# Products of 512 columns in two stages, norms' boundary chain reordered, broadcast and last values placed later

## The chip, the cores and the metric

The kernel runs on one core of one Trainium2 chip. Its time is the device time of one launch in microseconds. TensorE multiplies matrices, with stationary weights loaded ahead of each moving operand; ScalarE and VectorE prepare operands and empty PSUM, the banks into which TensorE writes; SyncE and GpSimd issue transfers.

## The reference

Two layers, each a mixer and a feed-forward block with norms before and after, on 16 meta tokens and 256 tokens of 2048 features:

```python
for layer in range(DEPTH):
    g = norm_g[layer]
    a = rms_norm(h, g[0])
    if layer % 2 == 0:
        ...   # u = a @ ab_w_in; mix = concat(pool_mixer, s5_mixer) @ ab_w_out
    else:
        ...   # mix = dsa_mixer(a, c_w_in, c_w_out)
    h = h + rms_norm(mix, g[1])
    a = rms_norm(h, g[2])
    f = jnp.square(jax.nn.relu(a @ mlp_w1[layer])) @ mlp_w2[layer]
    h = h + rms_norm(f, g[3])
return h[:, N_META:]
```

rms_norm multiplies by 1/sqrt(mean of squares over the 2048 features + 1e-6) and by a gain. The feed-forward width is 8192. dsa_mixer projects to 16 query heads of 128, 4 heads each of keys and values, 16 index queries of 64, one index key and 16 index weights; it rotates part of queries and keys, scores each query against all keys by the index parts, keeps the 64 best allowed keys, attends over them and projects back. All in float32.

## The kernel before

Activations lie with the features on 128 partitions, 16 chunks of 272 tokens (256 in the last feed-forward block and c_out, which leave the meta tokens out). Weights come as 684 tiles of 128x1024 float32, 512 KB each. For each, Stream.next issues a transfer on SyncE's queue into one of four wraw buffers, ScalarE copies it to float32r (whi, line 82), and VectorE subtracts that to get the rest (wlo, line 83). Activations are split into a high and a low half in the same way (a, ao, f). A product is three matmuls, high by high, high by low and low by high (three, lines 181 to 183). linear walks over quarters q of the 2048 inputs and in each over groups g of 256 output features; a tile holds four chunks and both halves m of a group, so 24 matmuls. A group that takes one bank pair is an mm tile, the third and later ones of a set two sd tiles.

Each engine takes its instructions in the order in which the scheduler put them, by the order of the code and by the priorities (high_priority, issue_after).

Three residuals (residual, line 284) stand between the stages. In this text A is the one after the first mixer, B the one after the first feed-forward block, C the one after c_out. TensorE does four filler matmuls (busy, line 136; they appear twice as many in the trace, since a float32 matmul is two passes), the totals (line 232) that sum the squares over the partitions, seven fillers, then the broadcast (line 258), which spreads the root over all partitions by a diagonal matrix dg, and eight fillers. Between totals and broadcast stands the root's chain (rstd_from, line 236): a square root on ScalarE and five small operations on VectorE. Then quarter(q) adds the normalised output to h (rt, then h) and splits the next stage's activations chunk by chunk.

The norm before a stage needs the new h's squares. That stage's first set of three groups runs on activations without the root; the squares are summed on VectorE as the quarters come (sqacc), and after the set totals, root and broadcast follow in the middle of the stage, before any of its output is scaled (mlp, lines 341 to 348, and mixer1, the second mixer):

```python
with tc.high_priority(250):
    squares(4)
with tc.high_priority(60):
    ps = sums.totals(n // 4)
with tc.high_priority(250):
    r = keep_bcast(rstd_from(ps, n // 4), n // 4)
```

In the second mixer the first set are keys and half of the values (kv_out), then come the index keys, the index queries (products of 512 columns by tokens, lines 1046 to 1048), scores, the selection of 64 keys by steps of max and match_replace on VectorE (lines 1103 and 1104), the other values (line 998 transposes them), and four groups of queries with the heads' attention between them. The second stage of the last feed-forward block (tail) works by tokens with 512 columns.

## Time and profile before

| | us |
|---|---|
| median of 3 runs | 2201.54 (2201.02 to 2202.66) |
| profiled execution | 2202.15 |
| its span | 2200.4 |
| TensorE busy | 2161.2 (98%) |
| VectorE busy | 1283.2 (58%) |
| ScalarE busy | 1025.7 (47%) |
| DMA engines' mean share (q1) | 51.6% |

The mean granted clock of TensorE is 0.992 of full speed. The stages: first mixer to 320.7 us, boundary A, first feed-forward block to 1100.9, boundary B, second mixer with c_out to 1457.5, boundary C, last feed-forward block to 2191. A duration of a matmul in the trace includes its way through the array, and neighbours overlap; what one costs in a stream is the distance between starts. In the idle columns the time in brackets is what the engine stood before the row, with what released it.

### The profile page before, as it was taken

To read this page: it belongs to the slowest core of one execution; us is meant where nothing else is said; L and a number is where in the kernel's file an instruction comes from. 1 tells how busy PE (TensorE), PEld (TensorE's weight loads), DVE (VectorE), ACT (ScalarE), POOL (GpSimd) and SP (SyncE) were. 2 spreads that over 40 slices of the span, in tenths; PEclk is the share of its full clock that TensorE was granted. 3 is DMA by queue.
4 is the path that set the end of the run, shared out by engine and by line. 5 is a ranking of instruction groups with operands and counts; after the bars stand their busy time and mean duration, and the time that the engine had idled before them with its cause. 6 is when DMAs were issued, how large, how long until landed. Compare 5 with 4: busy or idle time off the path is not lost.

```text
span 2200.4 us, 38716 instructions
## 1 busy us (share of the span) xinstructions
PE 2161.2 (98%) x15974; PEld 2034.2 (92%) x15974; DVE 1283.2 (58%) x1938; ACT 1025.7 (47%) x1437; POOL 30.2 (1%) x62
## 2 busy tenths in 40 slices
PE   9998999999999999999999999999999999999998
PEld 9988899999999999999998788999889989989986
DVE  8988569544544554455495855467445545545544
ACT  6553556444443443344364455456444434434442
POOL 0111000000000000000000000000000000000000
PEclk9999999999999999999999999999999999999999
DMA  7766646555555555555355432547555555555553
GB/s 238 210 180 176 193 153 197 177 174 179 175 173 178 177 173 179 176 173 176 132 167 172 149 125 87 185 129 225 189 192 184 189 187 187 186 188 191 184 197 99
DMA packets 108736, 385.14 MB, mean 175 GB/s; under 512 B 12736, under 2 KB 14656, under 8 KB 108432
## 3 DMA queue, kind: packets, MB, share of 16 engines
q1 hardware_dynamic: 103008, 368.55, 51.6%
q0 software_dynamic: 3968, 12.75, 2.3%
q8 instruction: 125, 2.05, 0.4%
q10 hardware_dynamic: 1584, 1.38, 0.2%
q14 instruction: 51, 0.42, 0.1%
HBM read 375.35 MB, written 7.27 MB: 174 GB/s over the span
## 4 chain that ended last, share of the span: by engine, by line
PE 88%; DVE 6%; issue 3%; DMA 2%; ACT 1%; POOL 0%; SPq 0%; DVEq 0%; POOLq 0%; ACTq 0%
PE mm L183 24%; PE mm L182 24%; PE mm L181 24%; PE mm L1046 2%; PE mm L1047 2%; PE mm L1048 2%; DVE wlo L83 1%; PE sd L182 1%; PE sd L181 1%; PE sd L183 1%; DMA wraw<-wall 1%; DVE a L165 1%; DMA tz<-kd 1%; DVE h L158 1%; DVE rt L158 1%
## 5 line engine op out<-in xcount | busy, mean ns | idle before, releaser
L83 DVE TENSOR_TENSOR wlo<-wraw,whi 128x1024 fp32r<-128x1024 f32 (+1 forms) x685 | 833.4, 1218 | 732.0 <-ACT whi L82 731.2
L82 ACT ACTIVATE whi<-wraw 128x1024 fp32r<-128x1024 f32 (+1 forms) x685 | 722.2, 1055 | 981.0 <-PE mm L182 681.5
L181 PE MATMUL mm<-a,whi 128*128 128x272 f32 (+1 forms) x2608 | 746.1, 287 | 2.0 <-ACT whi L82 1.9
L183 PE MATMUL mm<-a,wlo 128*128 128x272 f32 (+1 forms) x2608 | 746.5, 286 | 0.9 <-DVE wlo L83 0.9
L182 PE MATMUL mm<-a,whi 128*128 128x272 f32 (+1 forms) x2608 | 744.3, 286 | 0.2
L181 PEld LDWEIGHTS mm<-a,whi 128*128 128x128 f32 x2608 | 490.5, 188 | 4.0 <-ACT whi L82 2.4
L183 PEld LDWEIGHTS mm<-a,wlo 128*128 128x128 f32 x2608 | 490.6, 188 | 2.0 <-DVE wlo L83 1.5
L182 PEld LDWEIGHTS mm<-a,whi 128*128 128x128 f32 x2608 | 490.7, 188 | 1.3 <-DVE a L165 0.9
L182 PE MATMUL mm<-f,whi 128*128 128x272 f32 x992 | 287.0, 289 | 0.0
L183 PE MATMUL mm<-f,wlo 128*128 128x272 f32 x992 | 285.7, 288 | 0.0
L181 PE MATMUL mm<-f,whi 128*128 128x272 f32 x992 | 283.1, 285 | 0.0
L183 PE MATMUL mm<-whi,f 128*128 128x512 f32 x480 | 189.4, 395 | 0.0
L181 PE MATMUL mm<-whi,f 128*128 128x512 f32 x480 | 189.3, 394 | 0.0
L182 PE MATMUL mm<-wlo,f 128*128 128x512 f32 x480 | 188.6, 393 | 0.0
L181 PEld LDWEIGHTS mm<-f,whi 128*128 128x128 f32 x992 | 187.3, 189 | 0.0
L183 PEld LDWEIGHTS mm<-f,wlo 128*128 128x128 f32 x992 | 186.4, 188 | 0.0
L182 PEld LDWEIGHTS mm<-f,whi 128*128 128x128 f32 x992 | 186.2, 188 | 0.0
L183 PEld LDWEIGHTS mm<-whi,f 128*128 128x128 f32 x480 | 90.2, 188 | 21.1
L182 PEld LDWEIGHTS mm<-wlo,f 128*128 128x128 f32 x480 | 90.3, 188 | 20.8
L181 PEld LDWEIGHTS mm<-whi,f 128*128 128x128 f32 x480 | 90.4, 188 | 20.4
L1046 PE MATMUL mm<-whi,a 128*128 128x512 f32 x192 | 77.7, 405 | 0.0
L1047 PE MATMUL mm<-wlo,a 128*128 128x512 f32 x192 | 76.2, 397 | 0.0
(272 smaller groups left out, 2118.9 us busy)
## 6 DMA issues: line engine op xcount, KB each, us to landing
wraw<-wall SPq DMA_DIRECT2D x683, 512.0 KB, 3.6
qd<-q POOLq DMA_DIRECT2D x8, 512.0 KB, 4.3
tz<-kd POOLq DMA_DIRECT2D x32, 128.0 KB, 6.2
h<-hT SPq DMA_DIRECT2D x7, 544.0 KB, 6.0
bc<-bc SPq DMA_DIRECT2D x8, 256.0 KB, 3.2
qr<-qd POOLq DMA_DIRECT2D x4, 512.0 KB, 6.1
qq<-qd POOLq DMA_DIRECT2D x4, 512.0 KB, 5.7
out<-acc SPq DMA_DIRECT2D x8, 256.0 KB, 2.7
```

The source lines that it names most:

```text
L82: nc.scalar.activation(out=hi[:, x], in_=src[:, x], func=AF.Copy)
L83: nc.vector.tensor_tensor(out=lo[:, x], in0=src[:, x], in1=hi[:, x].bitcast(F32), op=SUB)
L158: return vec.tensor_tensor(out=out, in0=in0, in1=in1, op=op)
L165: return vec.scalar_tensor_tensor(out=out, in0=in0, scalar=scalar, in1=in1, op0=op0, op1=op1)
L181: pe.matmul(out=o, lhsT=wh, rhs=ah, start=first, stop=False)
L182: pe.matmul(out=o, lhsT=wh, rhs=al, start=False, stop=False)
L183: st.last = pe.matmul(out=o, lhsT=wl, rhs=ah, start=False, stop=last)
L1046: pe.matmul(out=o, lhsT=ah[:, s], rhs=hi[:, w], start=q == 0 and i == 0, stop=False)
L1047: pe.matmul(out=o, lhsT=ah[:, s], rhs=lo[:, w], start=False, stop=False)
L1048: st.last = pe.matmul(out=o, lhsT=al[:, s], rhs=hi[:, w], start=False, stop=q == 7 and i == 1)
```

## The change

In the first stage of the last feed-forward block and in c_out (but for its last group) a product becomes two matmuls: high weights by both activation halves, which lie side by side, into 512 columns, and low weights by the high half into the first 256. ScalarE then copies the second 256 columns out and VectorE adds the first. At the residuals the four fillers before the totals go, the root's chain is written with the reciprocal of the mean instead of that of the root, and each h follows its rt. In the middle of the stages the last squares are put ahead of the last quarter's weights, and totals, root and broadcast are apart: the broadcast comes in the third quarter of group 3 (feed-forward), or after half of the index keys (second mixer), whose other half comes after kv_out. The last values' kv_out comes behind three quarters of the first queries.

```diff
+    def two(o, wh, wl, both, ah, first, last):
+        pe.matmul(out=o, lhsT=wh, rhs=both, start=first, stop=False, skip_group_check=True)
+        st.last = pe.matmul(out=o[:, :256], lhsT=wl, rhs=ah, start=False, stop=last, skip_group_check=True)
+    def linear(name, groups, kcs, actf, n, row0=0, col0=0, before=None, mid=None, m_outer=False,
+               wide=None):
...
+            c, ends = kcs[4 * q + i], (q == 0 and i == 0, q == nq - 1 and i == 3)
+            if wide:
+                two(pt.m(m), w[0][:, s], w[1][:, s], wide(c), actf(c)[0], *ends)
+            else:
+                three(pt.m(m)[:, :n], w[0][:, s], w[1][:, s], *actf(c), *ends)
...
-        vec.reciprocal(out=r, in_=s)
-        stt(t, r, -0.5, r, MULT, MULT)
-        tt(t, t, v, MULT)
+        vec.reciprocal(out=v, in_=v)
+        tt(r, s, v, MULT)
+        stt(t, s, -0.5, r, MULT, MULT)
         stt(r, t, 1.5, r, ADD, MULT)
...
+    def side_by_side():
+        x = [apool.tile([128, 8, T], F32R, name="a").rearrange("p (c s) t -> p c s t", s=2) for _ in range(4)]
+        return [[y[:, :, s, :] for y in x] for s in range(2)] + [x]
+    def chunk(hl, s, c, t0=0, n=None):
+        k = 16 // len(hl[s])
+        return hl[s][c // k][:, c % k, t0:t0 + (n or T - t0)]
...
-        busy(bt, 4, st.last.ins)
         ps = sums.totals(n // 4)
         busy(bt, 7, sums.end.ins)
...
-                tt(t, mix(c, k), (b if c < 2 else kept)[:, None, :].to_broadcast([128, k, n]), MULT)
-                d = tt(x, x, t, ADD)
+                with tc.issue_after(d[-1].ins) if d else nullcontext():
+                    tt(t, mix(c, k), (b if c < 2 else kept)[:, None, :].to_broadcast([128, k, n]), MULT)
+                d.append(tt(x, x, t, ADD))
                 for j in range(k):
...
+        def last_squares(q):
+            if q == 3:
+                for c in range(12, 16):
+                    sums.add(c, hx(c, t0))
+        def taken(g, pt, force=False):
+            o = {}
+            for (m, k, x), (_, _, y) in zip(pt.spans(n), pt.spans(n, 256 if wide else 0)):
+                if force or wide:
+                    o[g, m] = tmp.tile([128, 2, T], F32, name="rl", tag="t2", bufs=4)[:, :k, :n]
+                    copy(o[g, m], y if wide else x)
+                    if wide:
+                        tt(o[g, m], o[g, m], x, ADD)
+            return o
...
+        def out1(g, pt, raws, fh, fl):
+            raws = raws or taken(g, pt)
+            for m, k, x in pt.spans(n):
+                c = 2 * g + m
+                rb = r[0][:, None, :n].to_broadcast([128, k, n])
+                rl = raws[g, m] if raws else tmp.tile([128, 2, T], F32, name="rl", tag="t2", bufs=4)[:, :k, :n]
+                stt(rl, rl if raws else x, 0.0, rb, MAX, MULT)
...
-            sets = [[0, 1, 2]] + [[g] for g in range(3, 8)] if b == 0 else [[g] for g in range(8)]
-            for gs in sets:
-                pts = linear(w1, gs, range(16), aget, n, col0=b * 2048, before=squares if r is None else None)
+            if b == 0:
+                gs = [0, 1, 2]
+                pts = linear(w1, gs, range(16), aget, n, before=squares, mid=last_squares, wide=wide)
+                ps = ps1()
+                with tc.high_priority(250):
+                    root = rstd_from(sums.totals(n // 4, ps=ps), n // 4)
                 raws = {}
-                if r is None:
-                    for g, pt in zip(gs, pts):
-                        for m, k, x in pt.spans(n):
-                            raws[g, m] = tmp.tile([128, 2, T], F32, name="rl", tag="t2", bufs=4)[:, :k, :n]
-                            act.activation(out=raws[g, m], in_=x, func=AF.Relu)
-                    with tc.high_priority(250):
-                        squares(4)
-                    with tc.high_priority(60):
-                        ps = sums.totals(n // 4)
-                    with tc.high_priority(250):
-                        r = keep_bcast(rstd_from(ps, n // 4), n // 4)
                 for g, pt in zip(gs, pts):
-                    for m, k, x in pt.spans(n):
-                        c = 2 * g + m
-                        rb = r[:, None, :n].to_broadcast([128, k, n])
-                        if raws:
-                            rl = raws[g, m]
-                            tt(rl, rl, rb, MULT)
-                        else:
-                            rl = tmp.tile([128, 2, T], F32, name="rl", tag="t2", bufs=4)[:, :k, :n]
-                            stt(rl, x, 0.0, rb, MAX, MULT)
-                        act.activation(out=rl, in_=rl, func=AF.Square)
-                        split(fh[c // 8][:, c % 8:c % 8 + k, :n], fl[c // 8][:, c % 8:c % 8 + k, :n], rl)
+                    raws.update(taken(g, pt, True))
+                def spread(q):
+                    if q == 2:
+                        with tc.high_priority(250), tc.issue_after(st.last.ins):
+                            r.append(keep_bcast(root, n // 4, ps))
+                        for g, pt in zip(gs, pts):
+                            out1(g, pt, raws, fh, fl)
+                pt, = linear(w1, [3], range(16), aget, n, col0=0, before=spread, wide=wide)
+                out1(3, pt, None, fh, fl)
+            for g in range(4 if b == 0 else 0, 8):
+                pt, = linear(w1, [g], range(16), aget, n, col0=b * 2048, wide=wide)
+                out1(g, pt, None, fh, fl)
...
+        pts = linear("c_in", gs, range(16), aget, T, col0=2048, before=squares, mid=last_squares)
+        rbank, xbank = ps1(), ps1()
         with tc.high_priority(250):
-            squares(4)
-        with tc.high_priority(60):
-            ps = sums.totals(T // 4)
-        with tc.high_priority(250):
-            rb = keep_bcast(rstd_from(ps, T // 4), T // 4)
-        rq = small.tile([128, 2], F32, name="rq", bufs=1)
-        vec.tensor_copy(rq, rstd_from(sums.totals(128, META, 2), 128, 2))
+            root = rstd_from(sums.totals(T // 4, ps=rbank), T // 4)
+        xk = xbank[:, :T]
+        def index_keys(x):
+            hi, lo = st.next(("c_in", 1024 * x, 8, 4096, 80), 640)
+            for i in range(8):
+                ah, al = aget(8 * x + i)
+                three(xk[:80, :], hi[:, 80 * i:80 * i + 80], lo[:, 80 * i:80 * i + 80], ah, al,
+                      x == 0 and i == 0, x == 1 and i == 7)
+        index_keys(0)
+        with tc.high_priority(250), tc.issue_after(st.last.ins):
+            rb = keep_bcast(root, T // 4, rbank)
...
+        index_keys(1)
+        rq = small.tile([128, 2], F32, name="rq", bufs=1)
+        vec.tensor_copy(rq, rstd_from(sums.totals(128, META, 2), 128, 2))
+        tt(KI[0:64], xk[0:64, :], rb[0:64], MULT)
+        tt(KI[64:80], xk[64:80, :], rb[64:80], MULT)
...
-        kv_out(3, pt)
-        for _ in project(0):
+        first_queries = project(0)
+        for _ in range(3):
+            next(first_queries)
+        with tc.issue_after(st.last.ins):
+            kv_out(3, pt)
+        for _ in first_queries:
...
-            pt, = linear("c_out", [g], range(16), lambda c: ao[c], 256, m_outer=g == 7)
+            wide = None if g == 7 else lambda c: ao[c]
+            pt, = linear("c_out", [g], range(16), lambda c: (ao[c][:, 0], ao[c][:, 1]), 256, m_outer=g == 7, wide=wide)
             c = 2 * g
+            o = mix[c // 8][:, c % 8:c % 8 + 2, :256]
             for m in range(2):
-                sums.add(c + m, pt.m(m)[:, :256])
-                copy(mix[c // 8][:, c % 8 + m, :256], pt.m(m)[:, :256], scale=g_t[:, 1, 1, c + m:c + m + 1])
+                x = pt.m(m)[:, :256]
+                if wide:
+                    copy(o[:, m], pt.m(m)[:, 256:])
+                    tt(o[:, m], o[:, m], x, ADD)
+                    x = o[:, m]
+                sums.add(c + m, x)
+                copy(o[:, m], x, scale=g_t[:, 1, 1, c + m:c + m + 1])
...
-    a = act_tiles()
+    a = side_by_side()
     quarter = residual(1, 1, mix, sums, META, to_next(1, 2, a, META))
```

On TensorE in the middle of the last block's first stage; sd tiles are the set's third group, and the four matmuls with ones and sqacc are the totals, the one with dg the broadcast. Before:

```order
L181 MATMUL mm<-a,whi 128x256
L182 MATMUL mm<-a,whi 128x256
L183 MATMUL mm<-a,wlo 128x256
L232 MATMUL sd<-ones,sqacc 64x1 x4
L181 MATMUL sd<-a,whi 128x256
L182 MATMUL sd<-a,whi 128x256
...
L183 MATMUL sd<-a,wlo 128x256
L258 MATMUL sd<-dg,ones 128x256
L181 MATMUL sd<-a,whi 128x256
```

and after:

```order
L188 MATMUL sd<-a,wlo 128x256
L187 MATMUL sd<-a,whi 128x512
L242 MATMUL sd<-ones,sqacc 64x1 x4
L188 MATMUL sd<-a,wlo 128x256
L187 MATMUL sd<-a,whi 128x512
...
L188 MATMUL mm<-a,wlo 128x256
L269 MATMUL sd<-dg,ones 128x256
L187 MATMUL mm<-a,whi 128x512
L188 MATMUL mm<-a,wlo 128x256
```

Eighteen matmuls stand between totals and broadcast in the first piece and 43 in the second, 11 of the set and 32 of group 3.

On TensorE around the transposes of the last values (vt) in the query products. Before:

```order
L1046 MATMUL mm<-whi,a 128x512
L1047 MATMUL mm<-wlo,a 128x512
L998 MATMUL sd<-ident,vt 128x128 x2
L998 MATMUL sd<-ident,vt 16x128
L998 MATMUL sd<-ident,vt 128x128 x2
L998 MATMUL sd<-ident,vt 16x128
L1048 MATMUL mm<-whi,a 128x512
L1046 MATMUL mm<-whi,a 128x512
```

and after:

```order
L1096 MATMUL mm<-whi,a 128x512
L1097 MATMUL mm<-wlo,a 128x512
L1098 MATMUL mm<-whi,a 128x512
L1053 MATMUL sd<-ident,vt 128x128 x2
L1053 MATMUL sd<-ident,vt 16x128
L1053 MATMUL sd<-ident,vt 128x128 x2
L1053 MATMUL sd<-ident,vt 16x128
L1096 MATMUL mm<-whi,a 128x512
L1097 MATMUL mm<-wlo,a 128x512
```

Of the 96 query matmuls that follow the group's last product, 14 stand ahead of these transposes before, and 72 after.

On VectorE at boundary C, the root's chain from nv on, the diagonal and the first chunks (numbers are of tiles; acc is c_out's output). Before:

```order
L171 TENSOR_SCALAR nv_15906<-sd_15886 64x4
L241 RECIPROCAL nr_15908<-ns_15907 64x4
L165 SCALAR_TENSOR_TENSOR nt_15909<-nr_15908 64x4
L158 TENSOR_TENSOR nt_15909<-nt_15909,nv_15906 64x4
L165 SCALAR_TENSOR_TENSOR nr_15908<-nt_15909,nr_15908 64x4
L158 TENSOR_TENSOR dg_15916<-ident_96,nr_15908 64x256
L158 TENSOR_TENSOR rt_15943<-acc_14844,sd_15881 128x256
L158 TENSOR_TENSOR rt_15948<-acc_14844,sd_15881 128x256
L158 TENSOR_TENSOR h_3477<-h_3477,rt_15943 128x256
L158 TENSOR_TENSOR h_3477<-h_3477,rt_15948 128x256
L158 TENSOR_TENSOR rt_15954<-acc_14844,rb_15927 128x2x256
L165 SCALAR_TENSOR_TENSOR a_15879<-h_3477,g_t_89,a_15877 128x256 x2
```

and after:

```order
L171 TENSOR_SCALAR nv_15680<-sd_15660 64x4
L252 RECIPROCAL nv_15680<-nv_15680 64x4
L158 TENSOR_TENSOR nr_15682<-ns_15681,nv_15680 64x4
L165 SCALAR_TENSOR_TENSOR nt_15683<-ns_15681,nr_15682 64x4
L165 SCALAR_TENSOR_TENSOR nr_15682<-nt_15683,nr_15682 64x4
L158 TENSOR_TENSOR dg_15690<-ident_96,nr_15682 64x256
L158 TENSOR_TENSOR rt_15717<-acc_14818,sd_15659 128x256
L158 TENSOR_TENSOR h_3477<-h_3477,rt_15717 128x256
L158 TENSOR_TENSOR rt_15722<-acc_14818,sd_15659 128x256
L158 TENSOR_TENSOR h_3477<-h_3477,rt_15722 128x256
L165 SCALAR_TENSOR_TENSOR a_15655<-h_3477,g_t_89,a_15655 128x256
L158 TENSOR_TENSOR rt_15728<-acc_14818,rb_15701 128x2x256
```

The reciprocal takes nv now and not ns, each h stands behind its rt, and the low half a of the first chunk stands ahead of the third rt.

## Rows read from the trace of the kernel before

**Rows 1.** page, part 1: busy us (share of span) xinstructions of each engine

```profile
PE 2161.2 (98%) x15974; PEld 2034.2 (92%) x15974; DVE 1283.2 (58%) x1938; ACT 1025.7 (47%) x1437; POOL 30.2 (1%) x62
```

**Rows 2.** timeline of TensorE, narrow products: start us, duration us, engine, line, operation

```profile
2039.76 0.28 PE L181 MATMUL mm<-a,whi 128*128 128x256 f32 x1
...
2047.91 0.28 PE L181 MATMUL mm<-a,whi 128*128 128x256 f32 x1
```

**Rows 3.** timeline of TensorE, last feed-forward block's second stage

```profile
1579.61 0.40 PE L183 MATMUL mm<-whi,f 128*128 128x512 f32 x1
...
1595.59 0.40 PE L183 MATMUL mm<-whi,f 128*128 128x512 f32 x1
```

**Rows 4.** groups by form: busy us, mean ns | idle before, by releaser

```profile
L82 ACT ACTIVATE whi<-wraw 128x1024 fp32r<-128x1024 f32 x679 | 719.2, 1060 | 978.3 <-PE mm L182 681.5 <-PE mm L183 188.8 <-PE mm L1048 60.5
```

**Rows 5.** timeline of TensorE, first queries and the values' transposes

```profile
1225.62 0.40 PE L1046 MATMUL mm<-whi,a 128*128 128x512 f32 x1
...
1226.56 0.40 PE L1047 MATMUL mm<-wlo,a 128*128 128x512 f32 x1
1229.45 0.74 PE L998 MATMUL sd<-ident,vt 128*128 128x128 f32 x5 [2.50 <-DVE vt L158]
```

**Rows 6.** timeline of ScalarE, middle of the last block's first stage

```profile
1495.23 1.06 ACT L82 ACTIVATE whi<-wraw 128x1024 fp32r<-128x1024 f32 x1 [4.46 <-DMA wraw<-wall]
1496.20 0.58 ACT L343 ACTIVATE rl<-mm 128x512 f32<-128x512 f32 x1
```

**Rows 7.** timeline of VectorE in the query stage

```profile
1228.58 0.72 DVE L158 TENSOR_TENSOR vt<-mm,rb 128x544 f32<-128x544 f32 x1
```

**Rows 8.** timeline of VectorE, middle of the first block's first stage

```profile
361.29 1.22 DVE L83 TENSOR_TENSOR wlo<-wraw,whi 128x1024 fp32r<-128x1024 f32 x1 [1.16 <-ACT whi L82]
```

**Rows 9.** timeline of TensorE at boundary A

```profile
322.06 1.12 PE L232 MATMUL sd<-ones,sq 128*68 128x1 f32 x16
323.04 1.81 PE L141 MATMUL sd<-ones 128*128 128x128 f32 x14
```

**Rows 10.** timeline of ScalarE at boundary A

```profile
321.38 0.43 ACT L220 ACTIVATE sq<-acc 128x272 f32<-128x272 f32 x1 [0.51 <-DVE acc L158]
```

**Rows 11.** timeline of VectorE at boundary B

```profile
1102.05 2.49 DVE L83 TENSOR_TENSOR wlo<-wraw,whi 128x1024 fp32r<-128x1024 f32 x2 [0.48 <-ACT whi L82]
```

**Rows 12.** timeline of TensorE at boundary C

```profile
1457.46 1.05 PE L141 MATMUL sd<-ones 128*128 128x128 f32 x8
1458.45 0.63 PE L232 MATMUL sd<-ones,sqacc 128*64 128x1 f32 x8
...
1464.90 0.39 PE L182 MATMUL mm<-a,whi 128*128 128x256 f32 x1
```

**Rows 13.** timeline of ScalarE at boundary C

```profile
1457.66 0.38 ACT L220 ACTIVATE sq<-sd 128x256 f32<-128x256 f32 x1 [0.68 <-PE sd L183]
```

**Rows 14.** timeline of VectorE at boundary C

```profile
1460.34 0.15 DVE L171 TENSOR_SCALAR nv<-sd 64x4 f32<-64x4 f32 x1 [9.02 <-ACT ns L239]
1460.41 0.16 DVE L241 RECIPROCAL nr<-ns 64x4 f32<-64x4 f32 x1
1460.61 0.15 DVE L165 SCALAR_TENSOR_TENSOR nt<-nr 64x4 f32<-64x4 f32 x1
...
1462.43 0.75 DVE L158 TENSOR_TENSOR rt<-acc,sd 128x256 f32<-128x256 f32 x2 [0.84 <-PE sd L258]
```

**Rows 15.** timelines of TensorE at the totals in the middle of three stages

```profile
363.01 0.62 PE L232 MATMUL sd<-ones,sqacc 128*68 128x1 f32 x8 [1.41 <-DVE sqacc L158]
...
1141.08 0.62 PE L232 MATMUL sd<-ones,sqacc 128*68 128x1 f32 x8 [0.42 <-DVE sqacc L158]
...
1146.07 0.70 PE L258 MATMUL sd<-dg,ones 68*128 68x272 f32 x2 [0.76 <-DVE dg L158]
...
1498.03 0.60 PE L232 MATMUL sd<-ones,sqacc 128*64 128x1 f32 x8 [2.19 <-DVE sqacc L158]
```

**Rows 16.** stretches of the span: length, busy of PE PEld DVE ACT POOL, PEclk, DMA

```profile
364.00:368.00 4.00, 4.00 (x22) 4.00 (x22) 3.40 (x9) 2.53 (x4) 0.00 (x0) 0.57 0.88 280
```

More of the change, by code (lines that the diff above doesn't have):

```diff
@@ L183, in three @@
         st.last = pe.matmul(out=o, lhsT=wl, rhs=ah, start=False, stop=last)
-    def linear(name, groups, kcs, actf, n, row0=0, col0=0, before=None, mid=None, m_outer=False):
+    def two(o, wh, wl, both, ah, first, last):
[3 more added lines that the diff above has]
+               wide=None):
         pts = [Pair(i < 2 and not m_outer) for i in range(len(groups))]
@@ L224, in add, with totals @@
                 self.squares.append(sq)
-        def totals(self, w, t0=0, runs=4):
-            ps = ps1()
+        def totals(self, w, t0=0, runs=4, ps=None):
+            ps = ps or ps1()
             parts = [self.acc] + self.squares
@@ L259, in bcast, with keep_bcast @@
         return ps[:, :4 * w]
-    def keep_bcast(r, w):
+    def keep_bcast(r, w, ps=None):
         o = small.tile([128, T], F32, name="rb", bufs=2)
-        copy(o[:, :4 * w], bcast(r, w))
+        copy(o[:, :4 * w], bcast(r, w, ps))
         return o
@@ L295, in residual @@
         kept = small.tile([128, T], F32, name="rb", bufs=2)[:, :n]
+        d = []
         def quarter(q):
@@ L308, in quarter @@
                 if c == 0:
-                    st.hold = (first, a and a.ins, d.ins)
+                    st.hold = (first, a and a.ins, d[0].ins)
         return quarter
@@ L315, in mlp @@
         aget = acts(a, t0, n)
-        r = None
+        wide = (lambda c: a[2][c // 4][:, c % 4, :, t0:]) if len(a) == 3 else None
+        r = []
         sums = Sums(n, 0)
@@ L326, in squares @@
         def squares(q):
-            if q < 4:
-                quarter(q)
+            quarter(q)
             for c in range(max(0, 4 * q - 4), 4 * q):
                 sums.add(c, hx(c, t0))
+        def last_squares(q):
[18 more added lines that the diff above has]
+                stt(rl, rl if raws else x, 0.0, rb, MAX, MULT)
+                act.activation(out=rl, in_=rl, func=AF.Square)
+                split(fh[c // 8][:, c % 8:c % 8 + k, :n], fl[c // 8][:, c % 8:c % 8 + k, :n], rl)
         for b in range(4):
@@ L961, in squares, with last_squares @@
         def squares(q):
-            if q < 4:
-                quarter(q)
+            quarter(q)
             for c in range(max(0, 4 * q - 4), 4 * q):
                 sums.add(c, hx(c))
-        pts = linear("c_in", gs, range(16), aget, T, col0=2048, before=squares)
-        with tc.high_priority(250):
-            squares(4)
-        with tc.high_priority(60):
-            ps = sums.totals(T // 4)
-        with tc.high_priority(250):
-            rb = keep_bcast(rstd_from(ps, T // 4), T // 4)
-        rq = small.tile([128, 2], F32, name="rq", bufs=1)
-        vec.tensor_copy(rq, rstd_from(sums.totals(128, META, 2), 128, 2))
+        def last_squares(q):
+            if q == 3:
+                for c in range(12, 16):
+                    sums.add(c, hx(c))
+        pts = linear("c_in", gs, range(16), aget, T, col0=2048, before=squares, mid=last_squares)
+        rbank, xbank = ps1(), ps1()
+        with tc.high_priority(250):
+            root = rstd_from(sums.totals(T // 4, ps=rbank), T // 4)
[9 more added lines that the diff above has]
+            rb = keep_bcast(root, T // 4, rbank)
         slot = resid.tile([128, 8 * T], F32, name="acc")
@@ L1004, in mixer1 @@
             kv_out(g, pt)
-        pt = pt2()[:, 0, :]
-        for x in range(2):
-            hi, lo = st.next(("c_in", 1024 * x, 8, 4096, 80), 640)
-            for i in range(8):
-                ah, al = aget(8 * x + i)
-                three(pt[:80, :T], hi[:, 80 * i:80 * i + 80], lo[:, 80 * i:80 * i + 80], ah, al,
-                      x == 0 and i == 0, x == 1 and i == 7)
-        tt(KI[0:64], pt[0:64, :T], rb[0:64], MULT)
-        tt(KI[64:80], pt[64:80, :T], rb[64:80], MULT)
+        index_keys(1)
[3 more added lines that the diff above has]
+        tt(KI[64:80], xk[64:80, :], rb[64:80], MULT)
         sw = at.tile([32, 4, T], F32, name="sw", tag="xs", bufs=2)
@@ L1107, in mixer1 @@
             tsc(s, s, -MASKED, None, MULT)
-        ao = [[at.tile([128, 256], F32R, name=f"ao{y}", tag="ao", bufs=32) for y in range(2)] for _ in range(NH)]
+        ao = [at.tile([128, 2, 256], F32R, name="ao", bufs=16) for _ in range(NH)]
         qts, lgs, pts = {}, {}, {}
```

16 lines of the change are left out of this document (6 added, 10 removed).

## Prediction

> **What bounds the kernel now.** I read the busy shares first, then the starts of consecutive products, then the waits at the boundaries between the stages, since only there does TensorE stand. TensorE is busy 98% of the span, VectorE 58% and ScalarE 47% [rows 1], so time is won only by fewer or shorter TensorE slots or by closing a wait of TensorE. The reader is to see in the two product timelines that TensorE never pauses inside a stage: 69 steps between products of 256 columns take 2047.91 - 2039.76 = 8.15 us, 118.1 ns each [rows 2], and 69 steps between products of 512 columns take 15.98 us, 231.6 ns each [rows 3]. The weights are there in time: of the 978.3 us in which ScalarE stood before a weight copy, 681.5 ended on a product that freed a weight buffer [rows 4], so the splits run as far ahead as the buffers let them. What is left are three residual boundaries, three norm totals in the middle of a stage and one wait on VectorE, all below.
>
> The profiled execution took 2202.15 us (span 2200.4 and 1.75 around it), 0.61 above the median of 2201.54. The terms are gains in that execution; I take them from the median.
>
> **The wide products.** Where the moving operand has 256 columns, a product's first two matmuls share their weights: high weights by high activations, and by low ones. The change makes them one of 512 columns, into two halves of a bank. Three steps of 118.1 (354.3 ns) become one of 231.6 and one of 118.1 (349.7): 4.6 ns less, since 512 columns cost a little under twice 256. The first stage of the last feed-forward block has 4 x 8 groups x 16 chunks x 2 halves = 1024 such products, c_out's first seven groups 7 x 32 = 224, together 1248: 1248 x 4.6 = 5.7 us. No 512-column product of before has its columns in two runs 272 apart, as they lie in the feed-forward stage. Bounds: the query products of 512 columns make four steps in 0.94 us [rows 5], 235 ns each against 2 x 118.1 = 236.2, which saves 1.5 us; and at the other end a step 0.5% (1.2 ns) shorter than in rows 3 saves 7.2. I take 5.7: rows 3 are the longest stretch, and their weights change at every step too.
>
> The Trainium skill's page "TensorE: Matmul & The Clock Gate" has two prices for this, in its section "Back-to-back issue gap": a real stream of weight loads and matmuls settles at about 131 ns for N = 512, and a single warm matmul takes N/2.4 + 2.5 ns. By the second, a removed matmul is worth 2.5 ns, 3.1 us in all. The first is far from this trace's 231.6; what it would mean is rival 5.
>
> Each wide group adds work behind it: ScalarE copies the second half out of the bank (0.58 us for 128x512 [rows 6]) and VectorE adds the first (0.72 for the like [rows 7]). A feed-forward group lasts 96 x 118.1 ns = 11.3 us, in which VectorE has four weight splits of 1.22 [rows 8], 4.9 us, and two operations of the like of 0.72; with the add it is at some 7 of 11.3. Both hide under the next group's products while weights stay ahead. If that cover is gone, they cost up to 0.58 + 0.72 = 1.3 us a group.
>
> **Residual boundaries A (before the first feed-forward block), B (before the second mixer), C (before the last block).** Eight filler matmuls before the totals go. At A the gain is cut by the late square, which ends on ScalarE at 321.38 + 0.43 = 321.81 [rows 10]; half of the last run of totals (323.04 - 322.06 = 0.98 [rows 9]) comes after it, so they can end at 322.3 instead of 323.04: 0.7. At B VectorE is in two weight splits from 1102.05 until 1104.5 [rows 11] and takes the chain's first operation only then: earlier totals change nothing. At C the fillers' 0.99 (1457.46 to 1458.45 [rows 12]) go whole, for the late square ends at 1458.04 [rows 13], before its totals are due: 1.0.
>
> The reordered root chain counts against this. Before, the reciprocal ran 0.07 behind the first operation, beside it; after, five operations hang on each other, and the first still stands behind the square root on ScalarE. One dependent step is 0.20 (1460.41 to 1460.61) [rows 14], so a boundary gets 0.20 - 0.07 = 0.13 longer, not shorter. Only at the kernel's end is the first operation placed without that wait; a step runs there beside the root: 0.2 won.
>
> The residual's multiply and add now alternate (a chunk's add right after its multiply, not after both multiplies), so the first normalised chunk comes one operation earlier, half of 0.75 [rows 14]; A and B win about 0.35 by that. At C a wide product needs the low half of its chunk at once, where before high products ran ahead until it came at 1464.90 [rows 12]; that takes back the 0.35 and, I estimate, 0.2 more (bounds: +0.2, and -0.8 for two operations' wait). Sum: A 0.7 - 0.13 + 0.35 = 0.9, B 0.2, C 1.0 - 0.13 - 0.2 = 0.7.
>
> **The totals in the middle of three stages.** Here TensorE waits for the last sum of squares on VectorE: 1.41 us at 363.01, 0.42 at 1141.08, 2.19 at 1498.03 [rows 15]. In the last feed-forward block this sum stood behind a weight split, whose copy ScalarE had begun only at 1495.23 after 4.46 us of waiting for its DMA [rows 6]. The change puts the last squares ahead of the last quarter's splits, and VectorE's sum comes after the first of them alone. The totals have eleven matmuls of the set behind them, 5 x 231.6 + 6 x 118.1 ns = 1.9 us, and the broadcast stands 43 matmuls, some 7.5 us, behind the totals. I expect 0.2 of wait to stay: 2.0 (bounds 0.5, if the split before it is as late, and 2.3). In the second mixer the totals stand five matmuls later, 0.6 us against the wait of 0.42, and the broadcast 54 matmuls behind the totals instead of 28, which ends its wait of 0.76 [rows 15]. With 0.15 at each that the idle column does not hold, for the restart, and another 0.1 for the second totals of this place: 1.6 (bounds 0 and 2). Behind the waiting instructions stand there the index keys and then the transposes of the values; a wait that moves onto these costs 0.76 again. In the first feed-forward block VectorE's sum still stands behind the split of 361.29 to 362.51 [rows 8], whose own wait of 1.16 is for ScalarE's copy. TensorE reaches the totals 0.6 later and has done as much more, and the broadcast is far behind: 0.6 + 0.3 = 0.9. The clock falls after this wait, to 0.57 granted over 364 to 368 [rows 16], which holds stretches at both levels, 1.2 and 2.4 GHz; at 0.57 the four microseconds do the work of 2.3, so 1.7 is lost. Whether a shorter wait spares that, no row shows: bounds 0 and 2.5.
>
> **The last values.** In the query stage TensorE goes from the product of 1226.56 to the transposes of 1229.45 with 2.50 us idle [rows 5], for a scaling on VectorE at 1228.58 [rows 7] behind the selection's steps. After, the transposes that need it stand behind 72 of the 96 query products instead of 14, 58 x 0.235 = 13.6 us later; VectorE keeps its place in the order, so the wait goes: 2.5 (bounds 0, if VectorE's queue falls as far behind, and 2.7).
>
> **Sum.** 5.7 + 0.9 + 0.2 + 0.7 + 0.9 + 1.6 + 2.0 + 2.5 + 0.2 = 14.7 us, and 2201.5 - 14.7 = 2186.8, given as 2187.
>
> **Rivals.** (1) The 512-column product with two runs saves nothing. For it: the query's 235 ns; against it: 231.6 over 69 steps. The rest stays, 9 us: 2192.5. (2) The waits move and do not go: a transfer or VectorE sets when the last sum comes, and TensorE stands a few products later. For it: the 4.46 us for a DMA, and the first block's sum, which keeps its split; against it: the last block's sum no longer stands behind that transfer. Then the middle totals give 0.5, the residuals 1, the values 1, and with 5.7 that is 8: 2193.5. (3) Slower: the second half of the bank is emptied between the weight splits, each engine holds a split back, and TensorE waits for weights once in each of the 32 + 7 = 39 wide groups. From 14.7/39 = 0.38 us a group it cancels the sum, from (14.7 + 4.4)/39 = 0.49 the kernel is slower by more than 0.2%; at the full 1.3 it is 2186.8 + 51 = 2238. For it: new work on both engines in every group; against it: ScalarE's 681.5 us of waiting for freed buffers. (4) The change does not reach the boundaries and only the wide products count: 2201.5 - 5.7 = 2196. (5) Wide products overlap so far that one steps as fast as a narrow one: 118.1 ns less per product, 147 us, and with the other 9 it gives 2045. Against it: rows 3 and 5, where nothing of the kind happens. The page's 131 ns above lies close to this.
>
> **How the numbers follow.** Forecast 0.66, rival 1 0.10, rival 2 0.14, rival 3 0.05, rival 4 0.04, rival 5 0.01. A measurement of this kernel tells about 0.2%, 4.4 us, from no change: 2197.1 to 2205.9. The forecast and rivals 1, 2 and 5 lie under it; rival 4 and the small end of 3 are near it. Faster 0.88, same 0.08, slower 0.04. The forecast's own range is 2182, with a clock that stays up and every wait gone, to 2191. For 8 of 10 it goes on towards rivals 1 and 2: 2181 to 2195.5.
>
> **What would show it.** Right: steps of 0.23 and 0.12 in a wide product; no wait on VectorE over 0.5 before the totals in the last block and the second mixer; none at the values' transposes; the totals at A and C right behind the last product. The sum is wrong if the new 512-column steps are 0.24 or more, if TensorE's weight loads wait for ScalarE or VectorE once in each group, or if the chain at A and C lets the broadcast start as late as before.

## The result and the profile after

The changed kernel takes 2186.16 us (median of 4 runs, 2182.10 to 2187.44) against 2201.28 of the kernel before: 0.9925 of it, interval 0.9912 to 0.9938, so 15.1 us faster. The forecast was 2187, 14.7 faster. The profiled execution took 2187.44 us, the longest of the four; its span is 2185.7 us, 14.7 under that of the profile before.

The page of the changed kernel, its first part and four groups (columns as in [rows 1, 4]; PEld are TensorE's weight loads):

```profile
PE 2151.2 (98%) x14702; PEld 1969.9 (90%) x14702; DVE 1307.5 (60%) x1985; ACT 1045.3 (48%) x1480; POOL 30.2 (1%) x62
...
L187 PE MATMUL mm<-a,whi 128*128 128x512 f32 x992 | 347.6, 394 | 0.3 <-DVE a L165 0.3
...
L188 PE MATMUL mm<-a,wlo 128*128 128x256 f32 x992 | 276.9, 279 | 0.0
...
L187 PEld LDWEIGHTS mm<-a,whi 128*128 128x128 f32 x992 | 186.1, 188 | 44.8 <-issue 0.4 <-ACT whi L82 0.3
...
L183 PE MATMUL mm<-whi,f 128*128 128x512 f32 x480 | 189.5, 395 | 0.0
```

TensorE has 14702 instructions, not 15974, and is as full as before [rows 1]. The steps of the wide products, from its timeline in the last block:

```profile
1998.68 0.39 PE L187 MATMUL mm<-a,whi 128*128 128x512 f32 x1
1998.91 0.28 PE L188 MATMUL mm<-a,wlo 128*128 128x256 f32 x1
1999.02 0.40 PE L187 MATMUL mm<-a,whi 128*128 128x512 f32 x1
1999.26 0.28 PE L188 MATMUL mm<-a,wlo 128*128 128x256 f32 x1
1999.38 0.39 PE L187 MATMUL mm<-a,whi 128*128 128x512 f32 x1
```

Two products take 1999.38 - 1998.68 = 0.70 us. Over the stage a 512-column matmul steps to the next in 232.5 ns on average and a 256-column one in 117.3, 349.8 together against the 349.7 worked out from [rows 2, 3]. These 992 matmuls wait 0.3 us in all for VectorE's split of the activations, and their weight loads 0.3 us in all for ScalarE's weight copy, far from once in each group. By these steps rivals 1 and 5 fall.

On TensorE: boundary A, then boundary C, then the totals in the middle of the three stages, then the values' transposes. They stand against [rows 9, 12, 15, 5].

```profile
319.25 0.59 PE L242 MATMUL sd<-ones,sqacc 128*68 128x1 f32 x8
...
320.91 1.81 PE L141 MATMUL sd<-ones 128*128 128x128 f32 x14
```

```profile
1449.83 0.29 PE L183 MATMUL sd<-ao,wlo 128*128 128x256 f32 x1
1450.05 0.63 PE L242 MATMUL sd<-ones,sqacc 128*64 128x1 f32 x8
...
1456.32 0.47 PE L187 MATMUL mm<-a,whi 128*128 128x512 f32 x1 [0.27 <-DVE a L165]
```

```profile
360.01 0.62 PE L242 MATMUL sd<-ones,sqacc 128*68 128x1 f32 x8 [0.22 <-DVE sqacc L158]
...
1137.57 0.62 PE L242 MATMUL sd<-ones,sqacc 128*68 128x1 f32 x8 [1.63 <-DVE sqacc L158]
...
1488.20 0.63 PE L242 MATMUL sd<-ones,sqacc 128*64 128x1 f32 x8
```

```profile
1236.59 0.82 PE L1053 MATMUL sd<-ident,vt 128*128 128x128 f32 x6
```

At A and C the totals stand right behind the last product. In the middle of the first block they wait 0.22 us, in the last block not at all, and the transposes wait for nothing. But before the second mixer's totals the wait has grown from 0.42 to 1.63. The stretches between starts of named TensorE matmuls tell where each microsecond went. All are of profiled executions; "again" is a second profile of the same changed kernel, and "the first low-half product" is the first matmul with low weights (wlo):

| stretch, us | before | changed | again | forecast of the difference |
|---|---|---|---|---|
| first mixer, to its last product | 320.58 | 319.12 | 318.73 | 0 |
| A, to the first low-half product | 7.87 | 6.93 | 6.94 | -0.9 |
| first block, to its last product | 772.35 | 769.61 | 769.59 | -0.9 |
| B, likewise | 8.59 | 8.33 | 8.32 | -0.2 |
| second mixer, to the last value product | 114.01 | 115.71 | 113.92 | -1.6 |
| to the last query product | 123.36 | 120.67 | 120.67 | -2.5 |
| to c_out's last product | 110.59 | 109.47 | 109.35 | -1.0 |
| C, to the first low-half product | 7.78 | 6.79 | 6.78 | -0.7 |
| last block, to the last product | 725.45 | 719.00 | 718.94 | -6.7 |
| end | 9.83 | 10.07 | 10.07 | -0.2 |

### The profile page after: what moved, and what is told of

Same layout as the page of the kernel before. It is cut to its first block, busy times and chain, and to the rows that moved or that the text cites. A ratio compares the mean times of both kernels' runs of the same rounds, so it can differ in the third digit from the quotient of the medians.

```text
span 2185.7 us, 36146 instructions
## 1 busy us (share of the span) xinstructions
PE 2151.2 (98%) x14702; PEld 1969.9 (90%) x14702; DVE 1307.5 (60%) x1985; ACT 1045.3 (48%) x1480; POOL 30.2 (1%) x62
## 4 chain that ended last, share of the span: by engine, by line
PE 90%; DVE 4%; issue 3%; DMA 2%; ACT 1%; POOL 0%; SPq 0%; DVEq 0%; POOLq 0%; ACTq 0%
PE mm L183 18%; PE mm L182 18%; PE mm L181 18%; PE mm L187 13%; PE mm L188 7%; PE mm L1096 2%; PE mm L1097 2%; PE mm L1098 2%; PE sd L182 1%; PE sd L181 1%; PE sd L183 1%; DVE wlo L83 1%; DMA tz<-kd 1%; DVE a L165 1%; PE sd L1183 1%
## 5 line engine op out<-in xcount | busy, mean ns | idle before, releaser
L181 PE MATMUL mm<-a,whi 128*128 128x272 f32 x1600 | 464.0, 290 | 2.5 <-ACT whi L82 2.5
L183 PE MATMUL mm<-a,wlo 128*128 128x272 f32 x1600 | 463.9, 290 | 0.6 <-DVE wlo L83 0.6
L182 PE MATMUL mm<-a,whi 128*128 128x272 f32 x1600 | 462.8, 289 | 0.0
L187 PE MATMUL mm<-a,whi 128*128 128x512 f32 x992 | 347.6, 394 | 0.3 <-DVE a L165 0.3
L181 PEld LDWEIGHTS mm<-a,whi 128*128 128x128 f32 x1600 | 301.6, 189 | 3.8 <-ACT whi L82 2.7
L182 PEld LDWEIGHTS mm<-a,whi 128*128 128x128 f32 x1600 | 302.4, 189 | 0.5
L188 PE MATMUL mm<-a,wlo 128*128 128x256 f32 x992 | 276.9, 279 | 0.0
L187 PEld LDWEIGHTS mm<-a,whi 128*128 128x128 f32 x992 | 186.1, 188 | 44.8 <-issue 0.4
L183 PEld LDWEIGHTS mm<-whi,f 128*128 128x128 f32 x480 | 90.1, 188 | 21.1
```

What stands on the lines that cost most here:

```text
L181: pe.matmul(out=o, lhsT=wh, rhs=ah, start=first, stop=False)
L182: pe.matmul(out=o, lhsT=wh, rhs=al, start=False, stop=False)
L183: st.last = pe.matmul(out=o, lhsT=wl, rhs=ah, start=False, stop=last)
L187: pe.matmul(out=o, lhsT=wh, rhs=both, start=first, stop=False, skip_group_check=True)
L188: st.last = pe.matmul(out=o[:, :256], lhsT=wl, rhs=ah, start=False, stop=last, skip_group_check=True)
```

## Experiments

Each tells by these stretches more than by its time: in all twelve profiles of this section A and B repeat to 0.02 us where their code is the same, while the first mixer, whose products no edit touches, takes 317.65 to 321.27. Where no time is given, the kernel ran once.

**no_alternate**, **narrow**, **fillers_back**, **old_chain** (one edit of the changed kernel each):

```diff
-                with tc.issue_after(d[-1].ins) if d else nullcontext():
+                with nullcontext():
```

> The changed kernel with one thing undone: at the residuals an add into h no longer has to follow its own multiply before the next multiply starts. Theory 1 (the new order at boundary B leaves VectorE waiting 1.40 us for a copy of ScalarE that stands behind a weight copy without data, so the last sum of squares and the totals in the second mixer come late and the clock falls): the wait before those totals falls from 1.63 us to under 0.5, no half-clock stretch at 1138, the stretch from B's first totals to the third key group's last product shrinks by 2 to 3.5 us, while A's first low-half product comes 0.3 later; in all 1.5 to 3 us faster than the changed kernel, near 2184. Theory 2 (the last squares placed ahead of the last quarter make the totals late, whatever the order of the chunks): the wait of 1.6 stays and the time is 0.4 to 1 us longer than the changed kernel. Theory 3 (the late transfer of that weight tile is this run's accident): the wait differs from run to run and goes with no order.

2189.82 us (2187.66 to 2190.82), 0.9951 of before (0.9935 to 0.9967). A and B lengthen by 0.4 and C by 0.34. Its totals in the first block and in the second mixer, then ScalarE's weight copy behind B:

```profile
361.77 0.62 PE L242 MATMUL sd<-ones,sqacc 128*68 128x1 f32 x8 [1.39 <-DVE sqacc L158]
...
1141.91 0.62 PE L242 MATMUL sd<-ones,sqacc 128*68 128x1 f32 x8 [1.68 <-DVE sqacc L158]
```

```profile
1121.73 1.06 ACT L82 ACTIVATE whi<-wraw 128x1024 fp32r<-128x1024 f32 x1 [5.30 <-DMA wraw<-wall]
```

Theory 1 falls: the wait in the second mixer stays without the new order, 1.68. What is there in both kernels is a weight copy that has to wait for its transfer: it starts 21.4 us behind the start of B's last product in the changed kernel and 22.2 here. And in the first block the wait of 1.39 comes back, with a clock that falls at 363.8, which costs 2.7 us (772.32): the order of the chunks is what had won there.

```diff
-        wide = (lambda c: a[2][c // 4][:, c % 4, :, t0:]) if len(a) == 3 else None
+        wide = None
...
-            wide = None if g == 7 else lambda c: ao[c]
+            wide = None
```

> The changed kernel with three 256-column matmuls for every product again, the rest of the change kept. If the wide products are worth 4.6 ns each by their steps, the stage of c_out takes 1.0 us and the last block's first stage 4.7 us more than in the changed kernel, in all 5.7, about 2192. Rival 1 of the prediction (two runs of columns cost what the saving gives): no difference in these stages. Rival 3 (emptying the second half of a bank holds the weights back): the stages get shorter by more than 0.4 us a group without it.

2193.53 us (2189.30 to 2195.60), 0.9961 of before (0.9948 to 0.9974). c_out's stretch is 110.59, 1.12 longer, as worked out; the last block's is 726.11, 7.1 longer and not 4.7. The steps show where: from the matmul on the activations' high half to that on their low half, which here still lie side by side in one tile, 119.9 ns, against 117.7 in the kernel before. Rivals 1 and 3 fall.

```diff
+        busy(bt, 4, st.last.ins)
         ps = sums.totals(n // 4)
```

> The changed kernel with the four filler matmuls before the totals at A, B and C again. By the late squares the fillers cost 0.7 at A, 0 at B and 1.0 at C, so the stretch from the last product to the first low-half product grows by these. Rival: the clock or the late square hide them at all three and nothing changes.

A 7.60, B 8.32, C 7.67: the fillers cost 0.67, 0 and 0.88, against 0.7, 0 and 1.0 expected.

```diff
-        vec.reciprocal(out=v, in_=v)
-        tt(r, s, v, MULT)
-        stt(t, s, -0.5, r, MULT, MULT)
+        vec.reciprocal(out=r, in_=s)
+        stt(t, r, -0.5, r, MULT, MULT)
+        tt(t, t, v, MULT)
```

> The changed kernel with the root's chain of before: reciprocal of the root beside the first operation, then three. My working: the stretch from the first operation (nv) to the diagonal gets 0.13 us shorter at A, B and C, and the end after the last product is 0.2 longer or the same. Rival: the new chain is the shorter one, as its reciprocal does not wait for the square root, and the stretch gets 0.1 to 0.2 longer without it.

A 6.81, B 8.20, C 6.71: the old chain is 0.12, 0.13 and 0.08 shorter. The changed kernel's chain on VectorE at B is five steps in a row, nv to the diagonal 0.97 us, where before the reciprocal ran 0.07 behind nv [rows 14]:

```profile
1099.32 0.15 DVE L171 TENSOR_SCALAR nv<-sd 68x4 f32<-68x4 f32 x1
1099.51 0.17 DVE L252 RECIPROCAL nv<-nv 68x4 f32<-68x4 f32 x1
1099.71 0.16 DVE L158 TENSOR_TENSOR nr<-ns,nv 68x4 f32<-68x4 f32 x1
1099.91 0.16 DVE L165 SCALAR_TENSOR_TENSOR nt<-ns,nr 68x4 f32<-68x4 f32 x1
1100.10 0.16 DVE L165 SCALAR_TENSOR_TENSOR nr<-nt,nr 68x4 f32<-68x4 f32 x1
1100.29 0.44 DVE L158 TENSOR_TENSOR dg<-ident,nr 68x272 f32<-68x272 f32 x1
```

At the kernel's end the new chain is the shorter one, as the sum had it, but by less: from the last sum of squares (ss) to the first scaled output it takes 1.23 us in each profile with the new chain and 1.30 in each with the old one, 0.07 and not 0.2. The stretch of the end is longer in the changed kernel, 10.07 against 9.87, for something else. ScalarE's last square, here in the changed kernel and in narrow, whose chain is the same,

```profile
2177.12 0.63 ACT L468 ACTIVATE sq<-acc 128x512 f32<-128x512 f32 x1 [6.00 <-DVE acc L158]
```

```profile
2184.73 0.63 ACT L468 ACTIVATE sq<-acc 128x512 f32<-128x512 f32 x1 [5.72 <-DVE acc L158]
```

starts 0.37 us behind the end of the sum that it reads in the first and 0.09 behind it in the second. In the ten profiles with the new chain it is 0.37 in four and 0.09 or 0.10 in six, and the end is 0.3 longer in the four; why is not known.

**hold_quarters**:

```diff
+            if q:
+                st.hold = (len(st.plan), a and a.ins, d[-1].ins)
```

> The changed kernel, with the weight splits of the second to fourth quarter after each residual put behind the normalised copies of that quarter, on ScalarE and VectorE. Theory 3' (the totals in the second mixer are late since ScalarE's queue has a weight copy whose transfer has not landed ahead of the chunks' copies; the landing varies from 19.6 to 22.6 us after the boundary): the chunks no longer wait for the transfer, VectorE's stall of 0.85 to 1.4 us there goes, the wait before the totals falls under 0.5 and the clock stays up, so the stretch from B to the last key and value products is near 112.5 us against 115.7. Theory 1' (VectorE itself is full there and sets the totals): the wait stays over 1 us. Risk under both: weights come later to TensorE and it waits for them inside the set, which would lengthen A, B and C by 1 us each.

2184.55 us (2184.17 to 2184.88). The totals in the second mixer:

```profile
1135.00 0.62 PE L242 MATMUL sd<-ones,sqacc 128*68 128x1 f32 x8 [0.27 <-DVE sqacc L158]
```

The wait is 0.27, the clock does not fall there, the stretch is 112.98. Theory 3' holds, and theory 1' falls; counted from the start of B's last product, the copies start 19.2 to 22.2 us behind it, not 19.6 to 22.6. The risk did not come at the boundaries, but the last block is 0.8 longer and the first 0.3, and the time is not clear of the changed kernel's (0.9926 of before, 0.9909 to 0.9942).

**squares_last** and **early_bcast** (the last squares after the set again, and the same in the second mixer; the broadcast right behind the root):

```diff
-                pts = linear(w1, gs, range(16), aget, n, before=squares, mid=last_squares, wide=wide)
+                pts = linear(w1, gs, range(16), aget, n, before=squares, wide=wide)
                 ps = ps1()
                 with tc.high_priority(250):
+                    last_squares(3)
...
```

> The changed kernel with the last four squares of the new h taken after the set's last weights again, as in the kernel before, the broadcast still late. If their place is what shortened the wait of the last block (2.19 to 0.2) and of the first block (1.41 to 0.22), these waits return to 1 to 2 us, and in the first block the clock falls as well: 1 to 3 us longer in that block and 1.5 to 2 in the last. Rival: the later totals (five to eleven matmuls) and the chunks' order did it, and the waits stay under 0.5.

```profile
359.84 0.62 PE L242 MATMUL sd<-ones,sqacc 128*68 128x1 f32 x8 [0.23 <-DVE sqacc L158]
...
1487.18 0.63 PE L242 MATMUL sd<-ones,sqacc 128*64 128x1 f32 x8
```

No wait comes back; 769.63 and 718.95. The place of the last squares, to which the forecast gave 2.0 us in the last block, is worth nothing. With it theory 2 falls too: the second mixer's totals still wait 1.27 us.

```diff
                     root = rstd_from(sums.totals(n // 4, ps=ps), n // 4)
+                    r.append(keep_bcast(root, n // 4, ps))
...
-                        with tc.high_priority(250), tc.issue_after(st.last.ins):
-                            r.append(keep_bcast(root, n // 4, ps))
```

> The changed kernel with the broadcast issued right behind the root in the middle of the three stages. The prediction gives the late broadcast 0.3 in the first block, 0.9 in the second mixer and nothing in the last block: TensorE waits that much again before the matmul with dg, and these stages get longer by it. Rival: the scheduler finds as late a place for it and nothing changes.

```profile
367.41 0.72 PE L269 MATMUL sd<-dg,ones 68*128 68x272 f32 x2 [0.48 <-DVE dg L158]
...
1143.98 0.72 PE L269 MATMUL sd<-dg,ones 68*128 68x272 f32 x2 [0.61 <-DVE dg L158]
```

The waits before the matmul with dg come back: the first block is 0.75 longer, and in the second mixer TensorE waits 0.61. The last block is 0.25 longer.

**kv_early**:

```diff
-        first_queries = project(0)
-        for _ in range(3):
-            next(first_queries)
-        with tc.issue_after(st.last.ins):
-            kv_out(3, pt)
+        kv_out(3, pt)
+        first_queries = project(0)
```

> The changed kernel with the last values' output back ahead of the first queries. If VectorE's selection steps set the wait, TensorE waits 2.3 to 2.7 us again before the values' transposes and the stretch from the last value products to the last query product grows from 120.67 us by the same. Rival: the wait of before came of the earlier boundary's timing and does not come back, change under 0.5.

```profile
1224.48 1.11 PE L1053 MATMUL sd<-ident,vt 128*128 128x128 f32 x6 [2.37 <-DVE vt L158]
```

The wait of 2.37 is back, and this time the clock falls at 1224.9, so that the stretch is 124.83, 4.2 longer. In the kernel before, the wait of 2.50 at the same place had no fall behind it.

**alternate_only** and **narrow_apart** (the alternating order alone in the kernel before; the narrow products with the halves in separate tiles):

```diff
...
+                with tc.issue_after(ds[-1].ins) if ds else nullcontext():
+                    tt(t, mix(c, k), (b if c < 2 else kept)[:, None, :].to_broadcast([128, k, n]), MULT)
...
```

> The kernel before with the alternating multiplies and adds of the residual alone. Theory (VectorE works without a break from the first multiply to the last sum of squares, and its order decides whether a weight split with late weights stands ahead of that sum): A and B give 0.4 each, C 0.3; the gap on VectorE of 1.16 us ahead of the first block's last sum and the wait of 1.4 before the totals go, the clock stays up, and the first block takes 769.6 to 770 us instead of 772.35. Rival: the wait in the first block goes by the later totals and broadcast, which this kernel does not have, and 772.3 stays.

```profile
357.97 0.62 PE L232 MATMUL sd<-ones,sqacc 128*68 128x1 f32 x8 [0.23 <-DVE sqacc L158]
...
1135.66 0.62 PE L232 MATMUL sd<-ones,sqacc 128*68 128x1 f32 x8 [0.30 <-DVE sqacc L158]
...
1143.56 0.49 PE L181 MATMUL mm<-a,whi 128*80 128x272 f32 x1 [2.00 <-DVE nt L165]
...
1494.69 0.60 PE L232 MATMUL sd<-ones,sqacc 128*64 128x1 f32 x8 [1.82 <-DVE sqacc L158]
```

A 7.47, B 8.19, C 7.46, first block 770.30: 0.4, 0.4, 0.3 and 2.05 shorter, as the theory has it. In the last block the wait is still 1.82 [rows 15], so it is not the order of the chunks that took it away. The second mixer is 2.5 longer, with a new wait of 2.00 for the second root's chain and a fall of the clock at 1142.9.

```diff
...
-    a = side_by_side()
+    a = act_tiles()
```

> The changed kernel with three 256-column matmuls per product, and the activations of the last block in separate tiles as before. With the halves side by side the narrow steps were 118.87 ns against 118.11 before. If the layout does that, the last block takes 719.0 + 4.7 = 723.7 us here against 726.1 with halves side by side, and the steps are 118.1; if the rest of the change does, it stays at 726.

Last block 723.77, high-to-low steps 117.7: the wide products are worth 4.8 us there, and 2.3 of the 7.1 that narrow lost were the layout. In c_out, whose halves lie side by side too, narrow's stretch is that of the kernel before, 110.59: the layout cost nothing there.

**hold_b_old_chain** and **changed_again** (`if q and (layer, i) == (0, 3):` before the hold, with the old chain; the changed kernel as it is):

> The changed kernel with the root's chain of before and, at boundary B alone, the weight splits of a quarter behind that quarter's copies. From the single runs: chain 0.12 at A, 0.13 at B, 0.08 at C and 0.2 at the end, 0.5 in all; B to the last key and value products 113.0 instead of 113.6 to 115.7, 0.6 to 2.7. The last block keeps its 719.0 us (holding at C cost 0.8). 1.1 to 3.2 us faster than the changed kernel, near 2184; where a transfer is late in the changed kernel more, where it isn't less. Rival: with the weights held back at B, TensorE waits inside the set and it is no faster.

> The changed kernel once more, on the chip and with the runs of the kernel before that the version with the old chain is compared with: 15 us under the kernel before, and by this trace's landing of the weight transfer behind B a wait before the second mixer's totals of 0.2 to 1.7 us.

2184.64 us (2183.34 to 2185.03) and 2184.69 (2182.82 to 2187.74), 0.9920 (0.9906 to 0.9933) and 0.9922 (0.9909 to 0.9936) of before: no difference that a time shows. In the stretches from A to the last product hold_b_old_chain takes 1853.4 us, the changed kernel 1856.5 and 1854.5. The second profile of the changed kernel has again a wait of 1.44 before the second mixer's totals, but no fall of the clock there, 1.8 us less than the first.

## Why the prediction was right, and where not

**Wide products, 5.7.** Right in mechanism and size: c_out 1.12 against 1.03, the last block 4.8 against 4.7.

**Boundaries, 1.8.** A 0.94, B 0.26, C 0.99 in place of 0.9, 0.2 and 0.7. Fillers (0.67, 0, 0.88), chain (-0.12) and order (0.39, 0.37, 0.34) are each shown. At C the order pays as at A; the forecast took 0.55 off for the wide product's low half, and it cost 0.15, by narrow's C of 6.64. So rival 4 falls.

**First block, 0.9: mis-sized.** It gave 2.74. The step "VectorE's sum still stands behind the split" failed. The alternating order brought the sum ahead of that split, which alternate_only and no_alternate show from both sides; the wait went to 0.22, and the clock, left open there, did not fall: 2.05 by the order, 0.7 by the late broadcast.

**Second mixer, 1.6: wrong.** In the changed kernel's first profile it lost 1.7, in the second it won 0.1; this is rival 2, in this one place. The forecast looked at the last instructions before the totals and took the sum's time as given. VectorE is busy there from the first rt (the first multiply of the residual) to the last sum, 34 us in the kernel before without a gap; any stall in these 34 us moves the sum. In the changed kernel that run lasts from 1101.55 to 1137.43, 35.88 us with 34.38 busy (the DVE column, as in [rows 16]), and the stall is 19 us ahead of the sum:

```profile
1101.55:1137.43 35.88, 34.40 (x274) 34.03 (x272) 34.38 (x61) 24.09 (x45) 0.00 (x0) 1.00 0.43 141
```

VectorE and ScalarE at the stall:

```profile
1118.52 0.92 DVE L165 SCALAR_TENSOR_TENSOR a<-h,g_t,a 128x272 fp32r<-128x272 f32 x2 [1.40 <-ACT a L174]
...
1136.51 0.92 DVE L158 TENSOR_TENSOR sqacc<-sqacc,sq 128x272 f32<-128x272 f32 x2
```

```profile
1117.02 1.06 ACT L82 ACTIVATE whi<-wraw 128x1024 fp32r<-128x1024 f32 x1 [3.89 <-DMA wraw<-wall]
1117.98 0.92 ACT L174 ACTIVATE a<-h,g_t 128x272 fp32r<-128x272 f32 x2
```

ScalarE's queue has a weight copy ahead of two chunks' copies; it waits 3.89 for its transfer, and VectorE waits 1.40 for the chunks. The sum comes 1.4 later, TensorE waits 1.63, and the clock falls: 0.57 is granted over this window, which holds stretches at both levels, 1.2 and 2.4 GHz:

```profile
1138.00:1142.00 4.00, 4.00 (x23) 4.00 (x22) 2.96 (x9) 2.38 (x3) 0.00 (x0) 0.57 0.96 346
```

hold_quarters takes away what waits, and the wait is gone. Where the stall is absent (hold_quarters, hold_b_old_chain, fillers_back) the second mixer wins 1.0 to 1.3, so the 1.6 was high even so: no run shows the 0.15 for each restart or the 0.1 for the second totals apart.

The transfer itself is issued 15.7 to 15.8 us behind B's last product in the changed kernel and in all its variants but no_alternate (16.8) and the two that hold weights back. What differs is the time to landing, here of the changed kernel and of fillers_back (a window of the DMA view around the one issue; the last number is us to landing):

```profile
q8 instruction: 1, 0.02, 5.9%
...
wraw<-wall SPq DMA_DIRECT2D x1, 512.0 KB, 5.5
```

```profile
q1 hardware_dynamic: 87, 0.36, 53.5%
...
wraw<-wall SPq DMA_DIRECT2D x1, 512.0 KB, 3.3
```

In the nine profiles with the stall it lands 4.9 to 5.5 us after its issue, and each has a 16 KB packet of the queue that the profile calls instruction (q8) in flight meanwhile. In fillers_back, alternate_only and the kernel before it lands after 3.3 to 3.4, and no such packet is there. The same holds, less strictly, of all weight transfers behind A that start with none other in flight: without such a packet none of 335 takes over 4.4 us, and 18 of the 53 do in whose first 2.8 us one starts. So the packet goes with a late landing; that it is the cause is not shown, for no run moved it alone.

**Last block's totals, 2.0.** The size holds (725.45 - 723.77 = 1.7 without the wide products); the cause given does not: it is neither the squares' place, nor the chunks' order, nor the broadcast, nor the fillers, nor the width, each undone alone without the wait's return. The totals' higher priority, and the squares' place ahead of the emptying of the set's banks, were not tried alone. The traces say more. In the kernel before and in alternate_only, which both wait, the last sum stands behind the split of one weight tile, and that tile's transfer lands 5.2 and 5.5 us after its issue, with a q8 packet in flight. In no_alternate, narrow and narrow_apart the last sum still stands behind the split of the same tile, but the transfer lands after 3.2 to 3.3 us without such a packet (in narrow one starts as it lands), and TensorE waits 0 to 0.43. In the changed kernel the sum is ahead of that split, as the forecast had it (and so it is in squares_last, with the squares' old place), and the transfer lands after 3.2 as well. So the wait went at least in part with a late transfer that this change was not meant to touch: as far as that goes, luck. Why the transfer is in time stays open.

**Last values, 2.5.** Right: 2.69 won, and kv_early, which brings the wait back, loses 4.2 with its fall of the clock.

**The end, 0.2.** Mis-sized: 0.07 by the chain, and 0.3 lost to the later square.

**The sum** of 14.7 met 14.7 in the profile, partly by cancelling and, in the last block, partly by luck: the second mixer fell 3.3 us short of its forecast, the first block gave 1.8 more, and the first mixer 1.5 by no edit.

## What to carry over

Where an engine is busy without a break up to the instruction that another waits for, forecast its whole run, not the last instructions: a stall far ahead arrives in full. Look for an instruction that may wait for a transfer, in the queue ahead of work that is ready: here the same transfer took 3.3 us in some profiles and 5.5 in others. A wait that goes is not yet a cause that is found: undo each part alone, and see whether what the wait hung on is late in both kernels. Two matmuls on the same weights are worth joining by the steps of the two widths in the same kernel, here 4.6 ns each, if the operands can lie side by side.

## What had not been expected

The layout of a moving operand can change its step: in the last block, with the halves side by side in rows of one tile, the second of two 256-column matmuls on the same weights came after 119.9 ns instead of 117.7, and after 117.7 with them apart; in c_out, with another tile, nothing changed. And the clock is no sure price of a wait. Nine profiles wait 1.12 to 1.68 us before the second mixer's totals, and the clock falls behind two of these waits, of 1.42 and 1.63, and not behind the longest. After the 2.50 of the kernel before [rows 5] it did not fall, after kv_early's 2.37 it did. Runs of the changed kernel spread from 2182.1 to 2187.4 us with mean clocks of 0.995 and 0.992.
